# The opening stage of a two-layer decoder trunk: another order of its transfers, other sums of squares, and three products of zeros

## The chip, the cores and the metric

The kernel runs on one core of one Trainium2 chip. The metric is the device time of one execution in microseconds (us). Three runs of the kernel before took 1147.78, 1148.49 and 1148.76 us, so the median is 1148.49 us. The names of the engines are those of the profile: PE is TensorE (PEld its weight loads), DVE is VectorE, ACT is ScalarE, POOL is GpSimd, and SP is the engine whose queue issues the transfers here.

## What is computed

A sequence of 512 tokens of width 1024 goes through two layers. Both layers also attend to 256 fixed memory tokens, whose keys and values come from the normalised memory. Only the start of the computation is touched by the change:

```python
mem_n = rms_norm(mem, ln_mem)
for layer in range(DEPTH):
    h = rms_norm(x, ln_mix[layer])
    mkv = mem_n @ w_mem_kv[layer]
    mem_k = mkv[..., :MEM_W].reshape(b_sz, MEM_LEN, MEM_HEADS, MEM_DH)
    mem_v = mkv[..., MEM_W:].reshape(b_sz, MEM_LEN, MEM_HEADS, MEM_DH)
    if layer < N_A_LAYERS:
        mix_out, mem_q = gated_deltanet_mixer(h, gdn_w_in[a], gdn_conv[a], gdn_A_log[a], gdn_dt_bias[a], gdn_norm[a])
    else:
        ...
    x = x + jnp.concatenate([mix_out, mem_o], axis=-1) @ w_out[layer]
    x = x + swiglu(rms_norm(x, ln_ffn[layer]), w_gate_up[layer], w_down[layer])
```

Here `rms_norm(x, g)` is `x * rsqrt(mean(x * x) + eps) * g`. The gated-DeltaNet mixer needs, besides large projections of `h`, twelve narrow columns of `h` (the logits of its gates).

## The kernel before

Everything lies transposed: the width of 1024 is cut into eight blocks (k = 0 to 7) of 128 partitions, and tokens run along the free axis. `x` is 128x8x512 and `mem` 128x8x256. All large products work on pairs of fp32r tiles: a value is split into a rounded high part and the rest, and each product is done as three (high by high, low by high, high by low; `mm3`, line 206). Splitting a weight takes one ACT copy (`whi`) and one DVE subtraction (`wlo`, `split`, line 176). Splitting a block of memory takes an ACT copy with the gain as its scale (`mh`) and one DVE operation (`ml`, `split_gain`, line 180).

The opening stage is `mem_and_norm` (line 304), followed by `gates` (line 410). In it come, in this order of the program: the transfers, issued one after the other from SP's queue; the splits of the memory; `keys(0)` (48 products into the banks `pj`); the memory's root mean square; the same for `x`; `memory_columns`; `values(0)`; `keys(1)`; `values(1)` (48 products each); and `norm`, which scales `x` and splits it into `h` and `l`. The order within each engine is made by a scheduler from this order and the operations' needs, so an operation can be put ahead of others; once built, each engine takes its instructions strictly in that order.

The root mean squares are made by `rstd_of` (line 229): ACT squares each block into a tile `sq`, DVE adds the squares of two blocks, and PE multiplies each such sum by a tile of ones, accumulating four products in a bank `g`; ACT then takes a logarithm and an exponential of it (`rsqrt`, line 224) into `mr` (memory) or `xr` (x). These products are of plain fp32 tiles. The ones come with the constants, by a transfer that stands ahead of those of `x` (`fetch_constants`, line 297).

`norm` (line 372) does three operations for each k: DVE scales `x` in place by the gain and `xr`, ACT copies it into `h`, and DVE subtracts, which gives `l`. `gates` multiplies the scaled `x` by the narrow weights `wab`; ACT copies the result into `ab`, four small products of `ab` with a part of the constants turn it round into a bank `g`, and ACT and DVE make the gates from that (`z`, `l`, `gate`). After these come the projections of the mixer (`conv_tile`, line 464), which fill PE: 24 products 512 wide for each tile of weights.

Of the kernel before, what the change touches and what calls it, by code (L numbers as in the profile page):

```python
# [18 lines left out]
P = 128  # L19
# [26 lines left out]
C_ID, C_U, C_ONE, C_CAUS, C_BAND = 0, 128, 256, 384, 512  # L46
C_SEL, C_INV, C_SIGN = 768, 780, 781
C_N = 782
# [20 lines left out]
def constants():  # L69
# [4 lines left out]
    c[:, C_ONE:C_ONE + P] = 1.0  # L74
# [14 lines left out]
class Builder:  # L89
# [139 lines left out]
    def rstd_of(self, tiles, pool, out, after=None):  # L229

        ps = self.bank("g")[:, :tiles[0].shape[1]]
        for k in range(0, KD, 2):
            two = []
            for x in tiles[k:k + 2]:
                sq = self.t(pool, [P, x.shape[1]], F32, "sq", 6)
                two.append(sq)
                ins = self.square(sq, x)
                if after is not None:
                    self.nosync(ins, after)
            self.tt(self.nc.vector, two[0], two[0], two[1], ALU.add)  # L240
            self.mm(ps, self.ones, two[0], k == 0, k == KD - 2)
        self.rsqrt(out, ps, D)


# [33 lines left out]
    def load_constants(self, cp):  # L278
# [8 lines left out]
        self.ones = c[:, C_ONE:C_ONE + P]  # L287
        self.caus = c[:, C_CAUS:C_CAUS + P]
        self.band = c[:, C_BAND:C_BAND + 2 * P]
        self.one = c[:, C_ONE:C_ONE + 1]  # L290
# [13 lines left out]
    def mem_and_norm(self, ep):  # L304
# [5 lines left out]
        ml = self.t(ep, [P, KD, ML], F32R, "ml")  # L310
        self.use(LN_EXP)
        early = lambda src: self.load(src, ep, 6)
        raw = [self.t(ep, [P, D], F32, "wraw", 6)]
        for k in range(0, KD, 2):
            nc.sync.dma_start(mem[:, k:k + 2, :], a["memT"][:, k:k + 2, :])
            if k < 4:
                s = slice(k // 2 * T, (k // 2 + 1) * T)
                nc.sync.dma_start(raw[0][:, s], a["wmk"][0, 0][:, s])
        raw += [early(a["wmk"][0, 1])]
        self.fetch_constants()  # L320
# [4 lines left out]
        raw += [early(s) for s in (a["wmv"][0, 0], a["wmv"][0, 1])]  # L325
# [3 lines left out]
        raw += [early(s) for s in (a["wmk"][1, 0], a["wmk"][1, 1], a["wmv"][1, 0], a["wmv"][1, 1])]  # L329
        self.kept = {}  # L330
# [3 lines left out]
        mem_stats = lambda after: self.memory_stats(ep, mem, mr, after)  # L334

        def keys(layer):
            ps, ks = [], []
            for m in range(2):
                w = self.weight(None, nc.vector, raw[4 * layer + m], 1 if m + layer else 2)
                ps.append(self.bank("sc" if layer else "pj")[:, :ML])  # L340
                for k in range(KD):
                    self.mm3(ps[m], w, k, (mh[:, k, :], ml[:, k, :]), k == 0, k == KD - 1)
            if layer == 0:
# [947 lines left out]
```

## Time and profile before

| What | Value |
|---|---|
| Runs of the kernel before | 1147.78 to 1148.76 us, median 1148.49 us |
| Profiled execution: its own time | 1148.39 us |
| Profiled execution: span from first to last instruction | 1146.6 us |
| Instructions | 19668 |
| DVE, ACT, POOL busy over the span | 73%, 55%, 7% |
| Transfers | 152.83 MB, mean 133 GB/s |

The profiled execution is 0.10 us below the median, so sums made against its trace can be set against the median as they are. The span is 1.8 us shorter than the execution's own time; what lies around it is taken to stay. A row of the timeline gives the start in us, the time that the merged instructions took together, engine, line, operation, what is written and read, shapes, and how many instructions follow each other; a bracket tells how long the engine had been idle before and what ended that. A row of the busy times by stretch gives the stretch, its length, and for PE, PEld, DVE, ACT and POOL the busy time and the number of instructions, then the granted TensorE clock, the share of the DMA engines and their rate. Matmuls overlap, so what one product costs is the distance between two starts, not its own length.

In this profile the first transfer of the memory lands before 5.45 us, the first product starts at 6.92 us, and the products of the gates start at 40.53 us.

### The profile page before, as it was taken

Reading aid. Unit: us, or ns where it says so; the run is one execution under the profiler, and the core shown is the slowest. Engines: PE = TensorE matmul, PEld = TensorE weight load, DVE = VectorE, ACT = ScalarE, POOL = GpSimd, SP = SyncE. Lnnn points to the kernel's source line nnn. Section 1 sums busy time; section 2 is a strip of 40 time slices with the busy share of each in tenths; the row PEclk is TensorE's granted clock in tenths of the full one; section 3 lists DMA queues with packets and bytes.
Section 4 is the critical chain, followed back from the end, with each engine's and each line's share of the span. In section 5 each row is a group of like instructions: output and inputs, shape, how many; then the busy total and the mean of one; then the engine's idle time right before and its main releaser. Section 6 shows DMA issues by size and latency. Waiting matters only on the chain.

```text
span 1146.6 us, 19668 instructions
## 1 busy us (share of the span) xinstructions
PE 1127.0 (98%) x7476; PEld 990.7 (86%) x7476; DVE 841.2 (73%) x1587; ACT 631.5 (55%) x1271; POOL 86.0 (7%) x97
## 2 busy tenths in 40 slices
PE   7999999999999999999999999999999999999996
PEld 5888887887899998899998777778999988999986
DVE  5764887766789987489866777759699843898754
ACT  7579572366556652256654556765566522566533
POOL 0220000000101100011100000010011100111000
PEclk9999999999999999999999999999999999999999
DMA  8333342325657744567723411144477733577232
GB/s 312 124 116 108 123 107 97 99 86 166 175 142 190 189 125 125 151 151 182 184 74 101 138 56 56 56 111 129 105 191 188 187 108 106 141 191 185 70 96 93
DMA packets 73972, 152.83 MB, mean 133 GB/s; under 512 B 17757, under 2 KB 18421, under 8 KB 73877
## 3 DMA queue, kind: packets, MB, share of 16 engines
q1 hardware_dynamic: 62356, 130.59, 36.8%
q0 software_dynamic: 11520, 20.98, 11.6%
q8 instruction: 59, 0.97, 0.4%
q14 instruction: 37, 0.30, 0.1%
HBM read 144.58 MB, written 6.96 MB: 132 GB/s over the span
## 4 chain that ended last, share of the span: by engine, by line
PE 89%; DVE 5%; ACT 4%; DMA 1%; issue 1%; SPq 0%; DVEq 0%; ACTq 0%
PE pj L154 44%; PE g L154 38%; PE sc L154 6%; ACT sm L142 2%; DVE wlo L161 1%; PE g L158 1%; DMA wraw<-in_wmk 1%; DVE q L161 0%; DVE sm L784 0%; PE qk L154 0%; ACT sm L148 0%; DVE l L164 0%; ACT whi L148 0%; ACT pf L148 0%; DVE l L161 0%
## 5 line engine op out<-in xcount | busy, mean ns | idle before, releaser
L148 ACT ACTIVATE whi<-wraw 128x512 fp32r<-128x512 f32 (+2 forms) x331 | 243.9, 746 | 244.9 <-PE pj L154 151.8
L161 DVE TENSOR_TENSOR wlo<-wraw,whi 128x512 fp32r<-128x512 f32 (+2 forms) x331 | 274.8, 840 | 102.6 <-ACT whi L148 96.8
L154 PE MATMUL pj<-h,whi 128*128 128x512 f32 (+1 forms) x676 | 267.4, 397 | 0.2 <-ACT h L148 0.2
L154 PE MATMUL pj<-l,whi 128*128 128x512 f32 (+1 forms) x676 | 264.2, 391 | 0.6 <-DVE l L164 0.4
L154 PE MATMUL pj<-h,wlo 128*128 128x512 f32 (+1 forms) x676 | 264.0, 390 | 0.0
L154 PE MATMUL g<-T,whi 128*128 128x256 f32 x1280 | 228.1, 278 | 0.2
L154 PEld LDWEIGHTS g<-T,whi 128*128 128x128 f32 x1280 | 194.7, 188 | 1.8 <-DVE fu L164 1.8
L154 PE MATMUL g<-T,wlo 128*128 128x256 f32 x640 | 177.8, 278 | 0.0
L154 PEld LDWEIGHTS pj<-h,whi 128*128 128x128 f32 x676 | 126.8, 188 | 31.2 <-issue 5.8
L154 PEld LDWEIGHTS pj<-l,whi 128*128 128x128 f32 x676 | 127.1, 188 | 26.8 <-issue 1.1
L154 PEld LDWEIGHTS pj<-h,wlo 128*128 128x128 f32 x676 | 127.0, 188 | 25.7 <-issue 0.3
L154 PE MATMUL g<-h,whi 128*128 128x256 f32 (+1 forms) x508 | 144.5, 285 | 0.0
L154 PE MATMUL g<-h,wlo 128*128 128x256 f32 (+1 forms) x508 | 144.3, 284 | 0.0
L154 PE MATMUL g<-l,whi 128*128 128x256 f32 (+1 forms) x508 | 144.2, 284 | 0.0
L154 PEld LDWEIGHTS g<-T,wlo 128*128 128x128 f32 x640 | 120.1, 188 | 0.0
L154 PEld LDWEIGHTS g<-h,whi 128*128 128x128 f32 x508 | 95.3, 188 | 1.5 <-issue 0.3
L154 PEld LDWEIGHTS g<-l,whi 128*128 128x128 f32 x508 | 95.3, 188 | 1.2
L154 PEld LDWEIGHTS g<-h,wlo 128*128 128x128 f32 x508 | 95.3, 188 | 1.1
L1025 POOL DMA_DIRECT2D ws<-in_wgu x40 | 35.4, 885 | 693.6 <-DMA ws<-in_wgu 274.9
L148 ACT ACTIVATE whi<-ws 128x512 fp32r<-128x512 f32 x80 | 50.5, 631 | 49.0 <-PE g L154 40.2
L161 DVE TENSOR_TENSOR fu<-pj,rstd 128x512 f32<-128x512 f32 (+1 forms) x34 | 22.4, 660 | 54.5 <-PE pj L154 54.4
L161 DVE TENSOR_TENSOR wlo<-ws,whi 128x512 fp32r<-128x512 f32 x80 | 54.9, 686 | 6.4 <-ACT whi L148 6.3
(355 smaller groups left out, 1617.9 us busy)
## 6 DMA issues: line engine op xcount, KB each, us to landing
wraw<-in_wgu SPq DMA_DIRECT2D x48, 512.0 KB, 4.3
ws<-in_wgu SPq DMA_DIRECT2D x80, 256.0 KB, 3.5
ws<-in_wgu POOLq DMA_DIRECT2D x80, 256.0 KB, 4.8
wraw<-in_wdn SPq DMA_DIRECT2D x48, 384.0 KB, 3.1
wraw<-in_win SPq DMA_DIRECT2D x26, 512.0 KB, 3.6
wraw<-in_wgu SPq DMA_DIRECT2D x40, 256.0 KB, 4.2
wraw<-in_wout SPq DMA_DIRECT2D x16, 512.0 KB, 3.6
wraw<-in_wdn SPq DMA_DIRECT2D x16, 256.0 KB, 2.7
```

The costliest lines, as they stand in the source:

```text
L142: ins = self.nc.scalar.activation(out, in_, func, **kw).ins
L148: self.copied = self.nc.scalar.activation(out, in_, AF.Copy, **kw).ins
L154: return self.nc.tensor.matmul(out, lhsT, rhs, start=start, stop=stop, skip_group_check=more).ins
L158: return self.nc.tensor.transpose(out, in_, self.ident[:k, :k]).ins
L161: return eng.tensor_tensor(out=out, in0=a, in1=b, op=op).ins
L1025: nc.gpsimd.dma_start(s1, a22, accum_op=ALU.add)
```

## The change

The order of the transfers becomes: gains, memory and the two weights of `keys(0)` (the second now in two halves), the weights of `values(0)`, `x`, `wab`, the weights of the second layer, and then the constants. The tile of ones is written on the chip by DVE, and no longer lies in the constants.

The memory's squares are made by POOL, four products of a tile with itself, 128x512 each, into tiles `mq`; DVE adds them up with four additions, and one product by ones follows where four stood. The squares of `x` are made by ACT in four operations of 128x1024, DVE adds them with seven additions, and again one product by ones follows; this one is put into `keys(1)`, after its fourth block. `norm` multiplies `x` by `xr` on POOL for k = 0, 2, 4, 6, 7 and on DVE for k = 1, 3, 5; the gain moves into the split (an ACT copy with a scale, a DVE operation with `x`, gain and `h`) and, for the gates, into `wab`, by one POOL product. Three products of a zeroed tile, 512 wide and of plain fp32, are put on PE ahead of everything else; POOL writes the zeros.

```diff
-    def rstd_of(self, tiles, pool, out, after=None):
-
-        ps = self.bank("g")[:, :tiles[0].shape[1]]
-        for k in range(0, KD, 2):
-            two = []
-            for x in tiles[k:k + 2]:
-                sq = self.t(pool, [P, x.shape[1]], F32, "sq", 6)
-                two.append(sq)
-                ins = self.square(sq, x)
-                if after is not None:
-                    self.nosync(ins, after)
-            self.tt(self.nc.vector, two[0], two[0], two[1], ALU.add)
-            self.mm(ps, self.ones, two[0], k == 0, k == KD - 2)
-        self.rsqrt(out, ps, D)
...
-        self.ones = c[:, C_ONE:C_ONE + P]
+        self.ones = self.t(cp, [P, P], F32, "ones")
+        nc.vector.memset(self.ones, 1.0)
...
+        zero = self.t(ep, [P, 2, T], F32, "sq", 4)[:, 0, :]
+        nc.gpsimd.memset(zero, 0.0)
+        for _ in range(3):
+            self.mm(self.bank("g"), zero[:, :P], zero)
         self.use(LN_EXP)
         early = lambda src: self.load(src, ep, 6)
-        raw = [self.t(ep, [P, D], F32, "wraw", 6)]
+        raw = [self.t(ep, [P, D], F32, "wraw", 6) for _ in range(2)]
+        half = [slice(i * T, (i + 1) * T) for i in range(2)]
         for k in range(0, KD, 2):
             nc.sync.dma_start(mem[:, k:k + 2, :], a["memT"][:, k:k + 2, :])
             if k < 4:
-                s = slice(k // 2 * T, (k // 2 + 1) * T)
-                nc.sync.dma_start(raw[0][:, s], a["wmk"][0, 0][:, s])
-        raw += [early(a["wmk"][0, 1])]
-        self.fetch_constants()
+                nc.sync.dma_start(raw[0][:, half[k // 2]], a["wmk"][0, 0][:, half[k // 2]])
+        for s in half:
+            nc.sync.dma_start(raw[1][:, s], a["wmk"][0, 1][:, s])
+        raw += [early(s) for s in (a["wmv"][0, 0], a["wmv"][0, 1])]
         for k in range(KD):
             self.split_gain(mem[:, k, :], self.gain(G_MEM, k), mh[:, k, :], ml[:, k, :])
         for k in range(0, KD, 2):
             nc.sync.dma_start(x[:, k:k + 2, :], a["xT"][:, k:k + 2, :])
-        raw += [early(s) for s in (a["wmv"][0, 0], a["wmv"][0, 1])]
         wab = self.wab = self.t(ep, [P, KD, 32], F32, "wab")
         nc.gpsimd.memset(wab, 0.0)
         nc.sync.dma_start(wab[:, :, 0:12], a["wab"])
         raw += [early(s) for s in (a["wmk"][1, 0], a["wmk"][1, 1], a["wmv"][1, 0], a["wmv"][1, 1])]
+        self.fetch_constants()
...
-        mem_stats = lambda after: self.memory_stats(ep, mem, mr, after)
-
-        def keys(layer):
+
+        def summed(pairs):
+            for i, j in ((0, 1), (2, 3), (0, 2)):
+                self.tt(nc.vector, pairs[i], pairs[i], pairs[j], ALU.add)
+            return pairs[0]
+
+        def squares_of_memory():
+            pairs = []
+            for k in range(0, KD, 2):
+                sq = self.t(ep, [P, 2, ML], F32, "mq", 4)
+                self.tt(nc.gpsimd, sq, mem[:, k:k + 2, :], mem[:, k:k + 2, :], ALU.mult)
+                pairs.append(sq)
+            both = summed(pairs)
+            self.tt(nc.vector, both[:, 0, :], both[:, 0, :], both[:, 1, :], ALU.add)
+            return both[:, 0, :]
+
+        def squares_of_x():
+            pairs = []
+            for k in range(0, KD, 2):
+                sq = self.t(ep, [P, 2, T], F32, "sq", 4)
+                self.square(sq, x[:, k:k + 2, :])
+                self.tt(nc.vector, sq[:, 0, :], sq[:, 0, :], sq[:, 1, :], ALU.add)
+                pairs.append(sq[:, 0, :])
+            return summed(pairs)
+
+        def rstd_of(sq, out):
+            ps = self.bank("g")[:, :sq.shape[1]]
+            self.mm(ps, self.ones, sq)
+            self.rsqrt(out, ps, D)
+
+        def keys(layer, between=None):
             ps, ks = [], []
             for m in range(2):
-                w = self.weight(None, nc.vector, raw[4 * layer + m], 1 if m + layer else 2)
+                w = self.weight(None, nc.vector, raw[4 * layer + m], 1 if layer else 2)
                 ps.append(self.bank("sc" if layer else "pj")[:, :ML])
                 for k in range(KD):
                     self.mm3(ps[m], w, k, (mh[:, k, :], ml[:, k, :]), k == 0, k == KD - 1)
+                    if between is not None and m == 0 and k == 3:
+                        between()
             if layer == 0:
-                mem_stats(self.copied)
+                rstd_of(squares_of_memory(), mr)
...
         def norm():
             self.h, self.hx = [], [x[:, k, :] for k in range(KD)]
+            self.tt(nc.gpsimd, wab, wab, self.gains[:, G_MIX[0]:G_MIX[0] + KD].unsqueeze(2).to_broadcast([P, KD, 32]), ALU.mult)
             for k in range(KD):
                 self.h.append(self.pair(self.apool))
-                xk = x[:, k, :]
-                self.stt(xk, xk, self.gain(G_MIX[0], k), xr, ALU.mult, ALU.mult)
-                self.split(xk, *self.h[k])
+                self.tt(nc.vector if k in (1, 3, 5) else nc.gpsimd, x[:, k, :], x[:, k, :], xr, ALU.mult)
+                self.split_gain(x[:, k, :], self.gain(G_MIX[0], k), *self.h[k])
 
         self.memK = keys(0)
-        self.rstd_of([x[:, k, :] for k in range(KD)], ep, xr)
         self.memory_columns(mr, mc)
         self.memV = values(0)
-        keys(1)
+        keys(1, lambda: rstd_of(squares_of_x(), xr))
         values(1)
         norm()
-
-    def memory_stats(self, ep, mem, mr, after):
-        self.rstd_of([mem[:, k, :] for k in range(KD)], ep, mr, after=after)
```

The rest of the diff renumbers the columns of the constants and drops `memory_stats`. Behind the gates no row differs on any engine, but that one projection product stands behind the small products of the gates and not ahead of them, and that `ones` is read where `consts` was.

On DVE, ahead of the product that needs the first weights' low parts, the order was this (numbers behind a name are the program's; `raw[1]` of the first layer is split in one piece):

```order
L161 TENSOR_TENSOR wlo_141<-wraw_91,whi_140 128x512
L164 SCALAR_TENSOR_TENSOR ml_89<-mem_86,gains_67,mh_88 128x256 x4
L161 TENSOR_TENSOR wlo_172<-wraw_98,whi_171 128x1024
L161 TENSOR_TENSOR sq_201<-sq_201,sq_203 128x256
L161 TENSOR_TENSOR sq_207<-sq_207,sq_209 128x256
L161 TENSOR_TENSOR sq_213<-sq_213,sq_215 128x256
L161 TENSOR_TENSOR sq_219<-sq_219,sq_221 128x256
```

With the change the same place reads as follows; `wlo_183` belongs to the second weight of `keys(0)`, `wlo_238` and `wlo_242` to those of `values(0)`:

```order
L163 SCALAR_TENSOR_TENSOR ml_91<-mem_88,gains_67,mh_90 128x256 x4
L160 TENSOR_TENSOR wlo_183<-wraw_102,whi_182 128x512
L160 TENSOR_TENSOR mq_213<-mq_213,mq_215 128x512
L160 TENSOR_TENSOR wlo_183<-wraw_102,whi_182 128x512
L160 TENSOR_TENSOR mq_217<-mq_217,mq_219 128x512
L160 TENSOR_TENSOR mq_213<-mq_213,mq_217 128x512
L160 TENSOR_TENSOR wlo_238<-wraw_111,whi_237 128x1024
L160 TENSOR_TENSOR mq_213<-mq_213 128x256
L160 TENSOR_TENSOR wlo_242<-wraw_113,whi_241 128x1024
```

The additions of the memory's squares now stand between the halves of the second weight and ahead of the weights of `values(0)`. POOL, which had only memsets before the mixer's `DT`, now has these rows in the opening stage:

```order
L296 MEMSET sq_92 128x512
L315 MEMSET wab_135 128x256
L160 ISA
L160 TENSOR_TENSOR mq_213<-mem_88 128x512
L160 TENSOR_TENSOR mq_215<-mem_88 128x512
L160 TENSOR_TENSOR mq_217<-mem_88 128x512
L160 TENSOR_TENSOR mq_219<-mem_88 128x512
L160 TENSOR_TENSOR wab_135<-wab_135,gains_67 128x256
L160 TENSOR_TENSOR x_89<-x_89,xr_150 128x512 x5
```

So nine products of 128x512 and one of 128x256 are new on POOL, five of them in the stretch of `norm`. On DVE the rows of that stretch were these, where `x` is scaled on DVE alone and weights of the second layer (`wlo_354`, `wlo_390`, `wlo_394`) stand among them:

```order
L164 SCALAR_TENSOR_TENSOR x_87<-x_87,gains_67,xr_139 128x512
L161 TENSOR_TENSOR wlo_354<-wraw_131,whi_353 128x1024
L161 TENSOR_TENSOR l_460<-x_87,h_459 128x512
L164 SCALAR_TENSOR_TENSOR x_87<-x_87,gains_67,xr_139 128x512
L161 TENSOR_TENSOR wlo_390<-wraw_133,whi_389 128x1024
L161 TENSOR_TENSOR kt_382<-sc_328,mr_137 128x256
L161 TENSOR_TENSOR l_465<-x_87,h_464 128x512
L161 TENSOR_TENSOR wlo_394<-wraw_135,whi_393 128x1024
L164 SCALAR_TENSOR_TENSOR x_87<-x_87,gains_67,xr_139 128x512
```

With the change they are these; the first `x` is k = 1, the two together are k = 3 and 5, and `wlo_571` belongs to the first projection of the mixer:

```order
L160 TENSOR_TENSOR wlo_384<-wraw_142,whi_383 128x1024
L160 TENSOR_TENSOR kt_376<-sc_303,mr_148 128x256
L160 TENSOR_TENSOR x_89<-x_89,xr_150 128x512
L160 TENSOR_TENSOR wlo_388<-wraw_144,whi_387 128x1024
L163 SCALAR_TENSOR_TENSOR l_450<-x_89,gains_67,h_449 128x512
L160 TENSOR_TENSOR kt_380<-sc_351,mr_148 128x256
L163 SCALAR_TENSOR_TENSOR l_455<-x_89,gains_67,h_454 128x512
L163 SCALAR_TENSOR_TENSOR l_460<-x_89,gains_67,h_459 128x512
L160 TENSOR_TENSOR x_89<-x_89,xr_150 128x512 x2
L160 TENSOR_TENSOR wlo_571<-wraw_568,whi_570 128x1024
L163 SCALAR_TENSOR_TENSOR l_465<-x_89,gains_67,h_464 128x512
```

The three `l` of k = 0, 1, 2 stand ahead of `x` for k = 3 and 5. On ACT, ahead of the copy of the gates' product (`ab`), stood this:

```order
L148 ACTIVATE kt_422<-sc_397,mc_138 128x256
L148 ACTIVATE whi_612<-wraw_610 128x1024
L148 ACTIVATE h_484<-x_87 128x512
L148 ACTIVATE h_489<-x_87 128x512
L148 ACTIVATE kt_451<-pj_426,mc_138 128x256
L148 ACTIVATE ab_503<-pj_494 128x512
L148 ACTIVATE z_510<-g_505 128x24
```

And now this, where `h_464` is k = 3, `h_474` is k = 5 and `h_484` is k = 7:

```order
L147 ACTIVATE whi_570<-wraw_568 128x1024
L147 ACTIVATE h_464<-x_89,gains_67 128x512
L147 ACTIVATE kt_416<-sc_391,mc_149 128x256
L147 ACTIVATE h_469<-x_89,gains_67 128x512
L147 ACTIVATE h_474<-x_89,gains_67 128x512
L147 ACTIVATE h_479<-x_89,gains_67 128x512
L147 ACTIVATE h_484<-x_89,gains_67 128x512
L147 ACTIVATE kt_445<-pj_420,mc_149 128x256
L147 ACTIVATE whi_607<-wraw_605 128x1024
L147 ACTIVATE ab_498<-pj_489 128x512
L147 ACTIVATE whi_659<-wraw_657 128x1024
L147 ACTIVATE z_505<-g_500 128x24
```

Five `h`, from k = 3 on, and one more weight (`whi_607`) now stand ahead of `ab`, where two `h` stood.

More of the change, by code (lines that the diff above doesn't have):

```diff
@@ L43 @@
 G_N = G_GDN + 1
-C_ID, C_U, C_ONE, C_CAUS, C_BAND = 0, 128, 256, 384, 512
-C_SEL, C_INV, C_SIGN = 768, 780, 781
-C_N = 782
+C_ID, C_U, C_CAUS, C_BAND = 0, 128, 256, 384
+C_SEL, C_INV, C_SIGN = 640, 652, 653
+C_N = 654
 INV_FREQ = [float.fromhex(s) for s in (
@@ L286, in load_constants @@
         self.U = c[:, C_U:C_U + P]
-        self.ones = c[:, C_ONE:C_ONE + P]
+        self.ones = self.t(cp, [P, P], F32, "ones")
+        nc.vector.memset(self.ones, 1.0)
         self.caus = c[:, C_CAUS:C_CAUS + P]
         self.band = c[:, C_BAND:C_BAND + 2 * P]
-        self.one = c[:, C_ONE:C_ONE + 1]
+        self.one = self.ones[:, 0:1]
         v = self.t(cp, [P, 10], F32, "eps")
```

1 line of the change is left out of this document (removed).

## The prediction

> **What bounds the kernel now.** I read the page first, then the busy times by stretch over the first 60 us, then the timeline there, engine by engine.
>
> ```profile
> PE 1127.0 (98%) x7476; PEld 990.7 (86%) x7476; DVE 841.2 (73%) x1587; ACT 631.5 (55%) x1271; POOL 86.0 (7%) x97
> PE 89%; DVE 5%; ACT 4%; DMA 1%; issue 1%; SPq 0%; DVEq 0%; ACTq 0%
> ```
>
> PE is busy 98% of the span and makes 89% of the chain that ended last. The rest of the chain is in the start:
>
> ```profile
> 0.00:10.00 10.00, 3.08 (x13) 2.85 (x14) 4.19 (x12) 5.33 (x10) 0.52 (x5) 1.00 0.71 237
> 10.00:20.00 10.00, 9.24 (x51) 7.26 (x51) 5.59 (x11) 8.48 (x21) 0.00 (x0) 1.00 1.02 370
> 20.00:30.00 10.00, 9.80 (x65) 8.07 (x65) 8.28 (x12) 8.34 (x14) 0.00 (x0) 1.00 0.73 287
> 30.00:40.00 10.00, 10.00 (x86) 10.00 (x85) 10.00 (x16) 6.23 (x9) 2.37 (x3) 1.00 0.12 40
> 40.00:50.00 10.00, 10.00 (x61) 6.93 (x60) 5.64 (x13) 4.46 (x13) 2.66 (x1) 1.00 0.54 161
> 50.00:60.00 10.00, 10.00 (x48) 8.12 (x47) 7.01 (x9) 6.83 (x15) 5.20 (x4) 1.00 0.67 231
> ```
>
> From 30 us on PE is busy 10.00 of every 10.00 us, and behind the gates no row of any engine is moved. So I take the shift of PE at the gates as the shift of the end, one for one. Between 30 and 40 us DVE too is busy 10.00 of 10.00: whatever is added to DVE, or holds it up, reaches the gates soon.
>
> ```profile
> 6.92 0.58 PE L154 MATMUL pj<-mh,whi 128*128 128x256 f32 x1 [6.92 <-ACT whi L148]
> 10.81 0.41 PE L154 MATMUL pj<-ml,whi 128*128 128x256 f32 x1
> 11.02 0.41 PE L154 MATMUL pj<-mh,wlo 128*128 128x256 f32 x1
> 11.81 0.28 PE L154 MATMUL pj<-ml,whi 128*128 128x256 f32 x1
> 11.93 0.28 PE L154 MATMUL pj<-mh,wlo 128*128 128x256 f32 x1
> 16.03 3.83 PE L154 MATMUL g<-sq,consts 128*128 128x256 f32 x12
> 20.31 2.29 PE L154 MATMUL g<-sq,consts 128*128 128x512 f32 x4
> 22.03 0.68 PE L154 MATMUL pj<-whi,mh 128*128 128x256 f32 x1
> 28.92 0.28 PE L154 MATMUL sc<-mh,whi 128*128 128x256 f32 x1
> 40.53 1.92 PE L154 MATMUL pj<-x,wab 128*32 128x512 f32 x16
> 43.42 0.95 PE L154 MATMUL g<-consts,ab 128*128 128x12 f32 x8
> 42.60 0.60 ACT L148 ACTIVATE ab<-pj 128x512 f32<-128x512 f32 x1 [1.01 <-PE pj L154]
> ```
>
> These are my milestones: the first product at 6.92, `keys(0)` done at 16.03, `values(0)` from 22.03 to 28.92, the gates' products at 40.53, the turning of `ab` at 43.42. Starts lie 0.21 apart at 11 us and 0.12 at 12 us, though the granted clock reads 1.00: PE begins at about half pace.
>
> **What the change removes on PE.** Eight products by ones become two. The twelve rows at 16.03 are four products of 128x256 and two of 128x512 (two rows each), as much as eight of 128x256 in 3.83 us: 0.48 each at most, and 0.43 less the drain of the last and a short wait. I take 0.43, and 0.86 for 128x512 (the 2.29 for two, at 20.31, has a wait and the drain in it). Six fewer are 3 x 0.43 + 3 x 0.86 = 3.9 us. If the zeros bring PE to full pace before 6.92, the 21 products up to 11.45 save 0.09 each, 1.9 us. With the 0.8 us that PE waited for the second `wlo`, some 6 us could go at best. That holds only if nothing else is late.
>
> **What it adds: POOL.** POOL read no tensor in this stretch; now it multiplies nine times 128x512. The trace has such work only later, and there it disturbs DVE:
>
> ```profile
> 54.80 1.30 POOL L161 TENSOR_TENSOR DT<-gcr,consts 128x512 f32<-128x512 f32 x1 [9.46 <-DMA gcr<-dr]
> 56.05 1.30 POOL L161 TENSOR_TENSOR DT<-gcr,consts 128x512 f32<-128x512 f32 x1
> 57.29 2.30 POOL L161 TENSOR_TENSOR DT<-gcr,consts 128x512 f32<-128x512 f32 x1
> 52.26 1.23 DVE L161 TENSOR_TENSOR wlo<-wraw,whi 128x1024 fp32r<-128x1024 f32 x1 [2.19 <-ACT whi L148]
> 56.38 2.05 DVE L161 TENSOR_TENSOR wlo<-wraw,whi 128x1024 fp32r<-128x1024 f32 x1 [0.66 <-ACT whi L148]
> 58.35 2.30 DVE L164 SCALAR_TENSOR_TENSOR kn<-pj,gains,kn 128x511 f32<-128x511 f32 x3
> ```
>
> `wlo` takes 1.23 us alone and 2.05 beside POOL. It ended at 58.43; less 1.23 it began at 57.20, when POOL's second operation (56.05 to 57.35) was ending. POOL's third took 2.30 for 1.30: it ended at 59.59, so began at 58.29, when `wlo` was ending. So they did not run together: they took turns, each starting some 0.14 before the other's recorded end. I therefore charge each such operation its duration less 0.13 on one common path. The three `kn` behind it, each with one input in a PSUM bank (`pj`), took 0.75 as ever while POOL went on. So the second input in SBUF seems to be what matters. DVE's new operations (`ml`, `l`, the additions, `x` by `xr`) have both inputs in SBUF; for additions and `x` the nearest row is `wlo` itself, for the three-operand `ml` and `l` no row shows it.
>
> [...]
>
> The durations:
>
> ```profile
> L148 ACT ACTIVATE whi<-wraw x14: 612/1054/1063, 6.3 to 55.3; 128x1024 fp32r<-128x1024 f32 x12, 128x512 fp32r<-128x512 f32 x2
> L161 DVE TENSOR_TENSOR wlo<-wraw,whi x14: 692/1226/2052, 6.9 to 56.4; 128x1024 fp32r<-128x1024 f32 x12, 128x512 fp32r<-128x512 f32 x2
> L164 DVE SCALAR_TENSOR_TENSOR ml<-mem,gains,mh x8: 478/480/486, 6.0 to 10.5; 128x256 fp32r<-128x256 f32 x8
> L164 DVE SCALAR_TENSOR_TENSOR x<-x,gains,xr x8: 746/747/751, 25.4 to 39.1; 128x512 f32<-128x512 f32 x8
> L161 DVE TENSOR_TENSOR l<-x,h x8: 684/689/693, 27.2 to 41.5; 128x512 fp32r<-128x512 f32 x8
> L148 ACT ACTIVATE h<-x x8: 613/616/635, 26.2 to 40.6; 128x512 fp32r<-128x512 f32 x8
> 5.45 0.91 ACT L148 ACTIVATE mh<-mem,gains 128x256 fp32r<-128x256 f32 x2 [3.43 <-DMA mem<-in_memT]
> 27.09 0.47 ACT L148 ACTIVATE mv<-pj,mc 128x256 f32<-128x256 f32 x1 [0.22 <-PE pj L154]
> 22.64 0.69 ACT L142 ACTIVATE xr<-g,eps 128x512 f32<-128x512 f32 x1 [0.94 <-PE g L154]
> ```
>
> On the common path, in us: POOL 1.16; `wlo` 1.10, its half 0.56; `ml` 0.35; an addition or `x` by `xr` 0.56; the new `l`, a three-operand one like the old `x`, 0.62. Two operations in a row on ACT lie their length less 0.08 apart.
>
> **Step 1, keys(0).** From 5.4 (the memory's first transfer, not moved) to the last `ml` the path carries 4 x 1.16 (squares), 8 x 0.35 (`ml`) and 2 x 0.56 (`wlo` of the first weight) = 8.6, with the tail of the last and small gaps 14.3. PE finishes the first weight's products at 14.9 and needs 24 x 0.12 = 2.9 for the second: 17.9, not 16.03. The first step is 1.8 us late, and PE's pace does not matter in it, since PE waits for `ml` and `wlo`: the zeros gain nothing here.
>
> **Step 2, values(0).** DVE then has two halves, three additions of 0.6, and `wlo` of the values: 18.6; one short addition, 19.0. The product by ones lies at 19.0 to 19.45; behind it stand 43 products of 0.12 and 0.45 for the memory's columns: 25.1, where before it was 28.92. Now 3.9 us are gained.
>
> **Step 3, keys(1) and values(1).** In ACT's order the copy `mv` of the last values stands ahead of the next weight: 0.2 + 0.47 + 1.05 after 25.1 gives 26.7, two products, then `x`'s one product by ones to 27.85. The low part of the weight waits for DVE's additions of `x`'s squares (ACT, busy with `mr` and `mv`, ends the squares at 24.8, and DVE adds until 26.9), takes 1.2 and comes at 28.1; 94 products of 0.12 then run to 39.4; before, 40.53. Of the gain 1.1 is left, since PE stood still for 1.7.
>
> **Step 4, x by xr.** `xr` waits for that product: logarithm to 28.65, one `whi` in between (0.97), exponential 0.6: 30.15, the path free at 30.75. From there it carries five POOL products (5.8), `x` for k = 1, 3, 5 (1.7), one `wlo` (1.1) and three `l` (1.85): 10.4, to 41.2. `x` of k = 3 comes at 40.8, of k = 5 at 41.4.
>
> **Step 5, ab.** ACT waits for k = 3. Then stand there five `h` (5 x 0.53), two `kt` (2 x 0.39), one `whi` (0.97), `ab` (0.62): 5.0, to 45.85. PE turns `ab` at 45.9, where before it was 43.42: **2.4 us later**. The 15 projections behind it (3.4) cover the gates' small chain (some 3.2 with `whi`, `wlo`, `z`). No more is lost, nothing regained.
>
> The transfers are not on this path: the memory and first weight keep their places, and constants, now last, are first read at the turning of `ab`; `x` can come 1.5 us later than before (18.5 for the last) without a change, as ACT squares it after 20. POOL's product on `wab`, half as large as the others, falls at about 20 us and costs DVE one short turn, if any. The memset of ones and the three products of zeros lie before 6.92, where PE and DVE waited. Sum: 1148.39 + 2.4 = **1150.8 us**. If the overlap of turns is 0.2 and not 0.13, steps 1 and 4 gain 1.2; if it is only 0.08, they lose 1.1. So the forecast's own range is 1149.5 to 1152.0.
>
> **Rivals.**
>
> *`ml` and `l` do not block* (only two-input operations without a scalar do). For it: no row shows them blocked. Against: they read two SBUF inputs at the same pace as `wlo`. Step 1 then ends at 15.1, `xr` comes at 27.4; the path carries 5.8 + 1.7 + 1.1 = 8.6 from 28.0, so `x` of k = 5 comes at 36.8; three `h`, `kt`, `whi` and `ab` give 40.4, and 0.6 goes at the gates, where `wlo` stands ahead of `z`. Result 2.4 faster, 1146.0 (1145.1 to 1147.9).
>
> *Nothing blocks*, POOL runs free, and the change does all that its words say: gates at 36.2, turning at 38.9; 4.6 faster, 1143.8. The 2.05 speaks against it.
>
> *DVE goes first* whenever it has an operation ready, so POOL waits. No row shows DVE with two such operations in a row beside POOL. Then `x` of k = 6 and 7 comes last, behind DVE's six `l` and `wlo` (13.4 on the path from 31.1: 45.0), with `h`, `kt`, `whi` and `ab` behind: 47.6, 4.0 later, 1152.4. It decides as soon as POOL's last `x` falls behind k = 5.
>
> *PE stays at or falls back to half pace* up to 18 us, because between 7 and 12 us it now waits more than it works: the second weight's products then take 5 and not 2.9; some of that falls into waits, and 1.1 is added: 1151.9.
>
> [...]
>
> **Numbers.** Chances: forecast 0.40, DVE first 0.16, half pace 0.10, `ml` and `l` free 0.27, nothing blocks 0.07. A measurement of this kernel can tell some 0.2%, 2.3 us, from no change: the bounds are 1146.1 and 1150.7. Half of the forecast lies above (0.20), with DVE first (0.16) and most of half pace (0.08): slower 0.44. Half of the forecast, the slower part of the first rival (0.11) and 0.02: same 0.33. The rest, 0.16 + 0.07, faster 0.23. The range takes in the forecast, both slower rivals and the first rival: 1145.2 to 1152.7; it leaves out mainly that nothing blocks.
>
> **What would show it.** In the changed profile `ml` and `l` with a mean well above 0.48 and 0.75 where POOL works, `wlo` up to 2.3: the common path. `keys(0)` done at about 18 tells step 1; `values(0)` done at 25 step 2; PE idle some 1.7 behind it step 3; POOL's five `x` stretched over about 9 us instead of 6.3, step 4; `ab` at 45 and idle PE ahead of the turning, step 5. I am wrong if `l` beside POOL takes 0.75, or if the gates come before 38; and I am wrong in the carrying over if PE idles somewhere behind 60 us.

## The result, and the profile after

| | before | changed |
|---|---|---|
| Median of four runs each | 1148.13 us | 1155.03 us |
| Lowest to highest | 1147.38 to 1148.76 | 1153.37 to 1156.12 |
| Ratio to before, 95% interval | | 1.0059 [1.0042, 1.0077] |
| Profiled execution: own time, span | 1148.39, 1146.6 us | 1153.37, 1151.5 us |

The change makes the kernel 6.9 us slower. The direction was forecast, the size was not: 1150.8 was given, with 1145.2 to 1152.7 as the range. The profiled execution is the fastest of the changed kernel's four, so its trace shows 5.0 of the 6.9 us.

The page first: busy times and the chain that ended last.

```profile
PE 1131.3 (98%) x7470; PEld 992.5 (86%) x7470; DVE 846.1 (73%) x1587; ACT 629.7 (55%) x1260; POOL 101.7 (9%) x108
PE 84%; DVE 8%; ACT 5%; issue 2%; DMA 1%; SPq 0%; DVEq 0%; ACTq 0%
```

PE's busy time grew by 4.3 us (1127.0 before), but the three products of zeros alone are 5.0 of that (first row of PE's timeline below), so the totals don't tell the cause. In the chain PE's share fell from 89% to 84% and DVE's rose from 5% to 8%: the end waits more for DVE. The stretches (busy time of PE, PEld, DVE, ACT and POOL, then the granted clock) say where:

```profile
10.00:20.00 10.00, 9.05 (x53) 8.70 (x54) 9.40 (x15) 4.89 (x8) 1.98 (x2) 0.70 1.05 395
40.00:50.00 10.00, 7.54 (x35) 4.58 (x30) 7.44 (x11) 6.46 (x11) 4.47 (x4) 0.83 0.43 133
```

The column of the granted clock, 1.00 in all six stretches before, falls to 0.70 between 10 and 20 us and to 0.83 between 40 and 50. PE is busy only 7.54 us of the latter, where it was 10.00 before. The timeline of PE shows both places:

```profile
1.32 5.01 PE L153 MATMUL g<-sq 128*128 128x512 f32 x6 [1.32 <-POOL sq L296]
...
11.96 0.58 PE L153 MATMUL pj<-ml,whi 128*128 128x256 f32 x1 [0.84 <-DVE ml L163]
...
18.62 0.59 PE L153 MATMUL g<-mq,ones 128*128 128x256 f32 x2
...
26.59 0.39 PE L153 MATMUL sc<-mh,whi 128*128 128x256 f32 x1 [1.51 <-ACT whi L147]
...
39.51 3.10 PE L153 MATMUL pj<-x,wab 128*32 128x512 f32 x16
...
46.06 1.34 PE L153 MATMUL g<-consts,ab 128*128 128x12 f32 x8 [2.32 <-ACT ab L147]
47.25 0.77 PE L153 MATMUL pj<-l,whi 128*128 128x512 f32 x1
47.82 0.63 PE L153 MATMUL pj<-h,wlo 128*128 128x512 f32 x1
...
49.95 0.46 PE L153 MATMUL pj<-l,whi 128*128 128x512 f32 x1
...
52.20 0.40 PE L153 MATMUL g<-consts,gate 128*24 128x128 f32 x2
...
61.31 0.66 PE L157 MATMUL g<-consts,kn 128*128 128x128 f32 x4
...
169.26 1.14 PE L153 MATMUL sc<-pf,mv 128*64 128x128 f32 x16 [0.56 <-ACT pf L147]
```

The milestones stand close to the forecast up to the turning of `ab`: product by ones 18.62 (forecast 19.0), first product of the next weight 26.59 (26.7), gates 39.51 (39.4), turning 46.06 (45.9). Then they part. Behind the turning the starts lie 0.43 apart (five products in the 2.13 from 47.82 to 49.95), where they lay 0.23 apart before (14 steps from 44.55 to 47.76). The products of `gate` stand at 52.20, before at 48.08: 2.64 late had become 4.12. (One projection product fewer stands ahead of them than before and follows behind them, so `kn`, at 61.31 for 56.92, is 4.39 late.) PE's rows of the kernel before at this place:

```profile
44.55 0.40 PE L154 MATMUL pj<-h,wlo 128*128 128x512 f32 x1
...
47.76 0.39 PE L154 MATMUL pj<-l,whi 128*128 128x512 f32 x1
48.08 0.40 PE L154 MATMUL g<-consts,gate 128*24 128x128 f32 x2
...
56.92 0.66 PE L158 MATMUL g<-consts,kn 128*128 128x128 f32 x4
```

DVE and POOL show what the prediction called the common path:

```profile
7.62 2.44 DVE L163 SCALAR_TENSOR_TENSOR ml<-mem,gains,mh 128x256 fp32r<-128x256 f32 x2
...
11.43 1.66 DVE L163 SCALAR_TENSOR_TENSOR ml<-mem,gains,mh 128x256 fp32r<-128x256 f32 x4
...
34.85 1.79 DVE L163 SCALAR_TENSOR_TENSOR l<-x,gains,h 128x512 fp32r<-128x512 f32 x1
...
39.97 1.28 DVE L160 TENSOR_TENSOR x<-x,xr 128x512 f32<-128x512 f32 x2
...
42.31 3.39 DVE L163 SCALAR_TENSOR_TENSOR l<-x,gains,h 128x512 fp32r<-128x512 f32 x5
...
51.95 0.18 DVE L163 SCALAR_TENSOR_TENSOR gate<-gate,ea 128x24 f32<-128x24 f32 x1
```

```profile
5.38 1.04 POOL L160 TENSOR_TENSOR mq<-mem 128x512 f32<-128x512 f32 x1 [3.87 <-DMA mem<-in_memT]
...
30.30 9.20 POOL L160 TENSOR_TENSOR x<-x,xr 128x512 f32<-128x512 f32 x5 [10.39 <-ACT xr L141]
```

`ml` took 1.22 each beside POOL's squares (two in 2.44) and 0.42 to 0.48 without them (four in 1.66); `l` took 1.79 beside POOL's `x`, and 0.68 each later. POOL's five products took 9.20 together, 1.84 each, where the first square took 1.04. So both sides wait. ACT, in turn, stood 5.04 us for `x` of k = 3, and later 2.30 for a transfer, with `z` behind it, so that `gate` was done only at 52.13 (51.95 and 0.18, last row of DVE above):

```profile
40.69 0.72 ACT L147 ACTIVATE h<-x,gains 128x512 fp32r<-128x512 f32 x1 [5.04 <-DVE x L160]
...
48.31 1.06 ACT L147 ACTIVATE whi<-wraw 128x1024 fp32r<-128x1024 f32 x1 [2.30 <-DMA wraw<-in_win]
49.27 0.17 ACT L147 ACTIVATE z<-g 128x24 f32<-128x24 f32 x1
```

### The profile page after: what moved, and what is told of

It reads as the page before. It is cut to its first block, busy times and chain, and to the rows that moved or that the text cites. A ratio compares the mean times of both kernels' runs of the same rounds, so it can differ in the third digit from the quotient of the medians.

```text
span 1151.5 us, 19664 instructions
## 1 busy us (share of the span) xinstructions
PE 1131.3 (98%) x7470; PEld 992.5 (86%) x7470; DVE 846.1 (73%) x1587; ACT 629.7 (55%) x1260; POOL 101.7 (9%) x108
## 4 chain that ended last, share of the span: by engine, by line
PE 84%; DVE 8%; ACT 5%; issue 2%; DMA 1%; SPq 0%; DVEq 0%; ACTq 0%
PE pj L153 40%; PE g L153 37%; PE sc L153 5%; ACT sm L141 2%; DVE wlo L160 2%; DVE l L163 1%; DVE btmp L160 1%; ACT whi L147 1%; DVE big L160 1%; ACT sm L147 1%; PE g L157 1%; DVE q L160 0%; DVE sm L799 0%; PE qk L153 0%; DMA big<-basein 0%
```

## The experiments

Each compares with runs of the kernel before on the same chip; "now" and "the changed kernel" in the expectations mean the changed kernel.

**POOL's reads, one by one and together.** Three kernels take POOL's products away, in `norm`, in the squares of the memory, and in both.

```diff
-                self.tt(nc.vector if k in (1, 3, 5) else nc.gpsimd, x[:, k, :], x[:, k, :], xr, ALU.mult)
+                self.tt(nc.vector, x[:, k, :], x[:, k, :], xr, ALU.mult)
```

> All eight products of x by xr go on DVE, POOL keeps the memory's squares. Theory (DVE and POOL take turns on operands in SBUF, and ACT, the gates and the chain behind ab are late because x of k = 3 and 5 is): from 31 us on l takes 0.75 each and wlo 1.2, the last x comes at about 42.3 (eight x of 0.6, six l of 0.66, one wlo and one kt from 31.3), ab is turned at about 43.7 and not at 46.06, ACT no longer stands idle for 5 us before h of k = 3, and the time falls by some 4 us against the changed kernel, to about 1151. Rival (DVE has simply too much to do there, the turns with POOL are not the cause): DVE has three more us of work, ab is turned after 47 and the time rises to 1157 or more.

Measured 1150.46 us, 1.0018 [1.0009, 1.0027]. DVE (first fence) and PE of this kernel:

```profile
39.72 0.75 DVE L163 SCALAR_TENSOR_TENSOR l<-x,gains,h 128x512 fp32r<-128x512 f32 x1
...
42.02 0.68 DVE L160 TENSOR_TENSOR x<-x,xr 128x512 f32<-128x512 f32 x1
```

```profile
44.50 1.06 PE L153 MATMUL g<-consts,ab 128*128 128x12 f32 x8
...
57.84 0.66 PE L157 MATMUL g<-consts,kn 128*128 128x128 f32 x4
...
166.08 1.14 PE L153 MATMUL sc<-pf,mv 128*64 128x128 f32 x16 [0.82 <-ACT pf L147]
```

With eight products on DVE in place of three, `l` takes 0.75, and the last `x` comes at 42.70 (42.02 and 0.68): 0.4 later than expected, and 1.45 later than DVE's last in the changed kernel (39.97 and 1.28). Yet `ab` is turned 1.56 earlier, at 44.50, since ACT is not held up by k = 3 with all its other work behind it: only one `h` and `ab` are left to it behind the last `x`. That order is new too. The scheduler, given this edit, also put projection products between those of the gates on PE, so what is gained belongs to the five products and the new order together. The rival, a turning after 47, is out. Turning and the transpositions of `kn` are late by 1.08 and 0.92 against before (43.42, 56.92): carried one to one, with no wait of 2.3 us in front. Another 1.16 went in two waits further on (0.82 here, 0.34 at 214.54), of which more below.

```diff
-                self.tt(nc.gpsimd, sq, mem[:, k:k + 2, :], mem[:, k:k + 2, :], ALU.mult)
+                self.square(sq, mem[:, k:k + 2, :])
```

> The memory's squares go on ACT, POOL keeps five products of x by xr. Theory (turns with POOL made keys(0) late): ml takes 0.48 each, the product by ones comes before 17 (now 18.8), values(0) ends near 23 (now 25.1), xr comes 2 us earlier, ab is turned near 44, and the time falls by 2 to 3 us against the changed kernel, to 1152 to 1153. Rival (the half pace of PE until 15.75 us, not POOL, made keys(0) late): ml is short, but products still lie 0.21 apart until 15 or so, and less than 1 us is gained. Second rival: what is gained at values(0) is lost again, since x by xr decides: ab turned at 46 as now, 1155.

Measured 1151.65 us, 1.0034 [1.0022, 1.0045], a little below the 1152 to 1153 expected. PE, and the stretch from 10 to 20 us:

```profile
15.95 0.64 PE L153 MATMUL g<-mq,ones 128*128 128x256 f32 x2
...
43.46 1.06 PE L153 MATMUL g<-consts,ab 128*128 128x12 f32 x8 [2.32 <-ACT ab L147]
...
45.20 0.63 PE L153 MATMUL pj<-h,whi 128*128 128x512 f32 x1
45.62 0.63 PE L153 MATMUL pj<-l,whi 128*128 128x512 f32 x1
...
58.66 0.66 PE L157 MATMUL g<-consts,kn 128*128 128x128 f32 x4
```

```profile
10.00:20.00 10.00, 9.43 (x71) 8.93 (x71) 9.55 (x16) 7.99 (x14) 0.62 (x1) 1.00 1.05 394
```

The product by ones comes at 15.95, the granted clock stays at 1.00, and `ab` is turned at 43.46: within 0.04 of the kernel before. Yet the kernel is 3.5 us slower than before. This row is the one that convicts the prediction's last step: the same 2.32 us of waiting ahead of the turning, products 0.43 apart behind it, and `kn` at 58.66 instead of 56.92 (1.3 of the span's growth to 1149.7 lies further on). A kernel that turns `ab` on time still loses what lies behind.

Both edits together:

> Both edits: no square of the memory and no x by xr on POOL. Theory: the two gains add, ab is turned near 41.5, the time is 1148 to 1149, at or a little above the kernel before; the rest of the new head is then worth nothing or 1 us. Rival (turns are not the cause): 1155 or more, as DVE and ACT have more work.

Measured 1147.54 us, 0.9996 [0.9987, 1.0005], a little below the expectation. The turning is 1.36 earlier than before:

```profile
42.06 1.06 PE L153 MATMUL g<-consts,ab 128*128 128x12 f32 x8
```

All that the changed kernel loses hangs on POOL's nine products of 128x512. Without them the new head is as fast as the old one, within what can be measured. That they do their harm by taking turns with DVE is what the rows of `ml`, `l` and POOL show; no kernel here has the products without the turns.

**The zeros.** Taken out of the changed kernel, and put alone into the kernel before.

```diff
-        zero = self.t(ep, [P, 2, T], F32, "sq", 4)[:, 0, :]
-        nc.gpsimd.memset(zero, 0.0)
-        for _ in range(3):
-            self.mm(self.bank("g"), zero[:, :P], zero)
```

> The changed kernel without the three products of zeros (and without the memset of their tile). Theory (PE waits for ml and wlo up to 14 us, so its pace does not matter there): first products 0.21 apart, all else where it was, keys(0) at 18, the time within 0.6 us of the changed kernel. Rival (the zeros warm PE to good purpose): keys(0) is 1 us later or more, the time 1 to 2 us longer. Second rival (the zeros bring the fall back of the clock forward, without them full pace starts earlier than 15.75): keys(0) before 17.5, the time 0.5 to 1 shorter.

Measured 1153.92 us, 1.0051 [1.0039, 1.0064]: its interval overlaps that of the changed kernel, with the middle 1 us below. The theory is not contradicted, a small cost of the zeros is not excluded.

```profile
18.41 0.59 PE L153 MATMUL g<-mq,ones 128*128 128x256 f32 x2
...
47.86 0.63 PE L153 MATMUL pj<-h,wlo 128*128 128x512 f32 x1
...
52.12 0.63 PE L153 MATMUL pj<-h,whi 128*128 128x512 f32 x1
```

The product by ones at 18.41 (18.62 with zeros): nothing is lost in the start without them. The same kernel shows a longer second stretch at half pace: products 0.43 apart from 47.86 to 52.12 at least, 4.3 us, where the profiled run of the changed kernel had 2.1.

> The kernel before with only the three products of a zeroed tile (and POOL's memset) put ahead. Theory (products lie 0.12 apart from 6.9 on, but the first weight's products end with the last ml at 11 and the second's wait for wlo until 13.3, so pace is worth little): 0.1 to 0.6 us faster than before, within 0.1%. Rival (pace matters): 1.5 to 2 us faster, about 1146.3. Rival (as in the changed kernel, PE falls back to half pace by 10 us because it waits too much): no gain at all or up to 1 us slower.

Measured 1148.11 us against 1148.45 on the same chip, 0.9997 [0.9988, 1.0006].

```profile
39.94 1.92 PE L154 MATMUL pj<-x,wab 128*32 128x512 f32 x16
```

The gates come at 39.94 for 40.53, 0.6 earlier, and that is all the zeros can do there.

**What lies behind the turning.** Two things end there at nearly the same time: 15 projections at half pace, and the gates' chain behind ACT's wait. Three kernels separate them. `fill` puts eight products into PE's wait (the other products are held at their places); `z_first` only changes the order of two operations; `fill_z` does both.

```diff
+        own = [self.mm(pt, self.h[0][0][:, :P], self.h[0][0]) for _ in range(8)]
         for c in range(NC):
-            self.mm(pt[:, c * 12:(c + 1) * 12], ab[:, c * P:(c + 1) * P], sel)
+            own.append(self.mm(pt[:, c * 12:(c + 1) * 12], ab[:, c * P:(c + 1) * P], sel))
+        self.pin[4] = own
```

> The changed kernel with eight more products of h by itself (128x512) on PE, into the bank that the turning of ab overwrites, between the fourth projection and the turning: 1.8 us of work in the 2.3 us in which PE waited. The order of every engine is otherwise the changed kernel's. In the changed kernel two things end together behind the turning: 15 projections at half pace (until 52.2) and the gates' chain (gate at 52.1, as ACT's z stands behind whi, which waits for a transfer until 48.3). Theory (both bind, each hides the other): projections 0.23 apart at once, but PE then waits over 1 us for the gate, whose products stay at 52.2; the profiled time is that of the changed kernel, 1153 to 1154, and only its slower runs go, so the median falls from 1155 by 1 to 1.5. Rival (the clock alone): the gate's products come at 50.7, median 1152 to 1152.5. Rival (the clock is not behind it): projections still 0.43 apart, no change.

Measured 1151.54 us, 1.0025 [1.0014, 1.0036], 3.5 below the changed kernel.

```profile
46.90 1.06 PE L154 MATMUL g<-consts,ab 128*128 128x12 f32 x8 [0.51 <-ACT ab L148]
47.82 0.48 PE L154 MATMUL pj<-l,whi 128*128 128x512 f32 x1
...
51.44 0.40 PE L154 MATMUL g<-consts,gate 128*24 128x128 f32 x2
```

The 15 projections take 3.62 (47.82 to 51.44) and not 4.95, and PE does not wait at the gate, which DVE had done just before, at 51.18:

```profile
51.00 0.18 DVE L164 SCALAR_TENSOR_TENSOR gate<-gate,ea 128x24 f32<-128x24 f32 x1
```

In this run the head up to the turning was 0.84 later than in the changed kernel's profiled run (46.90 for 46.06), and it is still 1.8 us shorter.

For `z_first`, `hold` is the copy into `z`, and `ins` the copy of the third weight:

```diff
-        self.copy(hi, src)
+        ins = self.copy(hi, src)
+        if self.hold is not None:
+            self.weights += 1
+            if self.weights == 3:
+                self.nosync(ins, self.hold)
```

> The changed kernel with ACT's z ahead of the third projection's whi (which waits for its transfer), and with the DVE operation that belongs to it moved likewise; PE, POOL and the transfers in the same order. Theory (both bind): z at 47.5, the gate ready by 49.7, but PE comes to the gate's products at 52.2 as before, as its 15 projections run at half pace; time within 0.5 us of 1155. Rival (the chain alone, the clock's pace being a result and not a cause): the gate's products at 50.7 or earlier, 1.5 us or more gained.

Measured 1154.94 us, 1.0054 [1.0041, 1.0067]: nothing. ACT's `z`, and PE:

```profile
47.52 0.19 ACT L149 ACTIVATE z<-g 128x24 f32<-128x24 f32 x1 [1.62 <-PE g L156]
```

```profile
47.33 0.78 PE L156 MATMUL pj<-l,whi 128*128 128x512 f32 x1
...
53.67 0.40 PE L156 MATMUL g<-consts,gate 128*24 128x128 f32 x2
```

`z` is 1.75 earlier (47.52 for 49.27), but the products of `gate` stand at 53.67: the 15 projections took 6.34.

> Both edits of fill and z_first. Theory (both bind): only now do the gate's products come early, at 50.7 or so, and the time falls to 1152 (3 below the changed kernel, of which 1.5 is the gate's and 1.5 the slower runs'). Rivals: the clock alone, the same as fill; the chain alone, the same as z_first.

Measured 1151.39 us, 1.0024 [1.0015, 1.0033]: the same as `fill`. My theory, that both bind and each hides the other, fell; the rival "the clock alone" holds. In `fill` the chain through `z` was done 0.26 before PE came. This depends on when ACT's transfer lands: in the changed kernel's profiled run it landed late and `gate` was done at 52.13, so PE at full pace, there by 50.87 (47.25 and 3.62), would have had to wait. In the four other traces with half pace behind the turning the chain was ready 0.9 to 3.4 us before PE came (`squares_act`, `warm_keys`, `no_zeros`, `z_first`), and there the pace alone binds.

**The first fall of the clock.** Eighteen small products between the first weight's, in the waits for `ml`.

```diff
                     self.mm3(ps[m], w, k, (mh[:, k, :], ml[:, k, :]), k == 0, k == KD - 1)
+                    if layer == 0 and m == 0 and k < 6:
+                        for _ in range(3):
+                            self.mm(spare, mh[:, k, 0:P], mh[:, k, :])
```

> The changed kernel with eighteen more products on PE (three of 128x256, of mh by itself into a bank that is free, behind each of the first six blocks of the first weight): 0.12 each, 2.2 us of work in the waits for ml between 7 and 12 us. All other orders are the changed kernel's. Theory (PE does not wait from 12 us on, so that the half pace until 15.75 does cost: 16 products by 0.09 are 1.5 us, of which DVE's last sum, ready at 17.7, lets 0.9 through): products 0.12 apart throughout, the product by ones at 17.7 or 17.8 and not 18.6, ab turned 0.9 earlier, time 0.5 to 1.2 below 1155. Rival (the prediction's step: PE waits, its pace is worth nothing): the product by ones at 18.6, no change.

Measured 1152.25 us (1150.25 to 1154.27), 1.0033 [1.0021, 1.0045].

```profile
17.96 0.67 PE L153 MATMUL g<-mq,ones 128*128 128x256 f32 x2
...
45.71 1.06 PE L153 MATMUL g<-consts,ab 128*128 128x12 f32 x8 [2.33 <-ACT ab L147]
46.62 0.48 PE L153 MATMUL pj<-l,whi 128*128 128x512 f32 x1
...
47.94 0.63 PE L153 MATMUL pj<-h,whi 128*128 128x512 f32 x1
```

The pace stays full (1.00 granted from 10 to 20 us), the product by ones comes at 17.96 (0.66 earlier), but the turning only 0.35 earlier, at 45.71. By this pair of runs the prediction's step was nearer to the truth than my 0.9; by another pair, `fill` and the next kernel, which adds these products to `fill`, the turning comes 0.89 earlier (46.90 and 46.01). The median fell by 2.8, more than either; what the profiled run shows beside the 0.35 is a second stretch at half pace that begins late: the five products from 46.62 to 47.94 take 1.32, full pace with a slow start, and only from 47.94 on they lie 0.43 apart. Runs of this kernel differ by 4 us, and the clock goes with them: the mean granted clock over a whole run was 0.997 and 0.998 in the two fastest (1150.25 and 1150.46), as in the kernel before, 0.995 in the profiled one and 0.992 in the slowest (1154.27). How much of the 2.8 belongs to the edit stays open.

> warm_keys and fill together: PE kept busy in both stretches in which it waited. Theory (the two losses add): about 0.9 below fill's 1151.5, 1150.6, which is then what POOL's turns alone cost. Rival: 1151.5 as fill.

Measured 1150.58 us, 1.0021 [1.0012, 1.0030].

```profile
46.01 1.06 PE L154 MATMUL g<-consts,ab 128*128 128x12 f32 x8 [0.50 <-ACT ab L148]
...
50.51 0.40 PE L154 MATMUL g<-consts,gate 128*24 128x128 f32 x2
...
59.58 0.66 PE L158 MATMUL g<-consts,kn 128*128 128x128 f32 x4
```

In the start this run still fell to 0.90 between 10 and 20 us; behind the turning it did not fall (1.00 from 40 to 60). The turning at 46.01 is 2.59 late against before, the gate 2.43, `kn` 2.66: nothing is added behind it. The time is 2.4 above the 1148.19 measured beside it.

**A version that beats both.** From `no_pool_reads`, with the gates taken off the path: `xr` is one factor for each token, so it can be applied to the result for the gates instead of to `x`.

```diff
+            self.gps = self.bank("pj")
+            for k in range(KD):
+                s = slice(32 * (k % 4), 32 * (k % 4 + 1))
+                self.mm(self.gps[s, :], wab[:, k, :], x[:, k, :], k < 4, k >= 4)
...
-        self.copy(ab, ps)
+        self.tt(nc.vector, ab, self.gps, self.xr, ALU.mult)
```

> No POOL product on memory or x (as in no_pool_reads), and the gates taken off the path through x by xr: their products read the raw x while PE waits ahead of keys(1), and DVE multiplies the 128x512 result by xr in place of ACT's copy into ab (xr is one factor for each token, so it may be applied behind the product). ab is turned right behind the values, the low part of the first projection's weight stands ahead of x of k = 3 or later on DVE, and the gate's products stand behind the 16th projection or later. Theory (what was left late in no_pool_reads is DVE's chain x, l, wlo ahead of the gates: ab turned at 42.1, first wlo product at 41.5): ab turned before 39, the 28th projection 3 us earlier than there, time 1144 to 1145.5. Rival (DVE's l bind, whatever the order): 1147 as before. Rival (PE waits thinly between 37 and 44, the clock falls back again): 1148 or more, with a wider spread.

Measured 1144.54 us, 0.9969 [0.9956, 0.9981]: as expected.

```profile
37.17 0.95 PE L156 MATMUL g<-consts,ab 128*128 128x12 f32 x8
```

The turning is at 37.17. PE waits twice further on, 1.58 us at 161.01 and 1.35 at 210.51, in this profiled run, which took 1146.03; the other four took 1143.96 to 1144.61 and have no trace.

> early_gates without the three products of zeros. Theory (zeros move the gates by at most 0.6 us, as in the kernel before): within 0.7 us of early_gates. Rival (with no waits for POOL the zeros pay): 1.5 to 2 us longer.

Measured 1143.07 us, 0.9958 [0.9944, 0.9971], the fastest of all: 5.4 below before. The rival, that the zeros pay here, is out. The theory missed too: 1.47 below `early_gates` is more than its 0.7, so the zeros seem to cost something here, of which the traces place 0.5.

```profile
36.63 0.95 PE L156 MATMUL g<-consts,ab 128*128 128x12 f32 x8
```

The first product starts at 6.75, not at 7.24 as with zeros, and the turning is 0.54 earlier.

## Why the prediction was wrong

**Step 1, keys(0): the number held, half of its working did not.** The product by ones came at 18.62 (19.0 given for it in step 2). The last product of the second weight started at 17.89, and 17.9 was forecast; but two errors cancelled there, which is luck. The last `ml` ended at 13.09, not 14.3: the first square took POOL 1.04 (first row of POOL above), and the sum had charged it like `DT`, with its 1.30; four times 0.26 are most of the 1.2. And PE, after its last wait (up to 11.96), worked at half pace up to 15.75, 0.21 for each product and not 0.12. "PE's pace does not matter in it" was therefore wrong as a mechanism; it cost 0.66 at the product by ones and 0.35 at the turning (`warm_keys`). That the zeros gain nothing was right (`no_zeros`, `before_zeros`).

**Steps 2 to 4 held.** Turns between POOL and DVE for `ml` and `l` are the point on which forecast and first rival differed. No row of the kernel before shows them; charging them was my estimate. Measured: 1.22 for 0.48, 1.79 for 0.75. `x` of k = 3 released ACT at 40.69 (40.8). DVE did not go first: POOL's last `x` ended at 39.50, ahead of DVE's for k = 3 at 39.97.

**Step 5 failed in its last sentence.** The turning came at 46.06, for 45.9. "The 15 projections behind it (3.4) cover the gates' small chain. No more is lost": the 15 took 4.95 (47.25 to 52.20) in the fastest run, and some 6.3 in another (47.33 to 53.67, `z_first`, whose PE order is the same). The chain was mis-sized as well: 3.2 was given for it, and it took 6.07 (46.06 to 52.13) in the changed kernel's profiled run and 3.80 to 5.20 in `warm_fill`, `warm_keys`, `fill`, `no_zeros` and `squares_act`, where `z` stands at the same place. The cause of the lost pace is the 2.32 us in which PE stood still ahead of the turning: with eight products in it (`fill`) the granted clock reads 1.00 from 40 to 60 us, and 0.83 from 40 to 50 without them. I had forecast that wait, named it as a sign, and carried its length one to one, without asking what it does to PE's clock. `fill` gives it a price of 3.5 us in the median; `squares_act` shows it with a turning that is on time. The traces place 3.2 of it where the half pace was long (`z_first`: turning and 15 projections 7.71 from 45.96 to 53.67, where `fill` has 4.54), and 1.6 in the changed kernel's fastest run (6.14), where the late `gate` would have taken most of that as well. The rival "half pace" was priced for the first stretch alone.

**The sum, term by term.** Turns and the late chain: 2.4 forecast, 2.4 measured with both waits filled (`warm_fill`). That these agree so well is in part luck, as `warm_fill` still fell to 0.90 in its start and carries 26 products more. The clock: 0 forecast; filling both waits gave 4.4 back (1155.03 less 1150.58), 3.5 of it by the wait ahead of the turning. The missing term is larger than the whole forecast. One addition among the rivals is off: in *DVE goes first*, 31.1 and 13.4 make 44.5, not 45.0; the forecast doesn't hang on it.

**"I am wrong in the carrying over if PE idles somewhere behind 60 us"**: it did, by 0.56 at 169.26. With 4.39 at `kn` (61.31 for 56.92) that makes up the 4.9 by which the span grew.

A wait of 2.32 or 2.33 us was enough for half pace behind it in four of four profiled runs that had it with nothing put in (0.83 granted between 40 and 50 us in `after` and `squares_act`, 0.82 in `no_zeros` and `z_first`), and in `warm_keys` with a delay (0.89, then 0.94 between 50 and 60). In the first 60 us the granted clock reads 0.50 in eleven stretches of nine traces, and each lasts 3.4 or 6.8 us. What sets these lengths is not shown.

## What to carry to other kernels

When an estimate makes PE wait for as long as it did here, allow for a slower pace behind the wait besides its length: filling this wait of 2.32 us gave 3.5 back. Look for small products that can stand in the wait; `z_first`, which only shortened the chain behind it, gave nothing. And moving five products of 128x512 to POOL relieved DVE of little: its last `x` ended at 41.25, and at 42.70 where DVE does all eight (`x_all_dve`). Beside each other DVE's `l`, which reads two SBUF tiles, took 1.79 and not 0.75, POOL's product 1.84 where the first square took 1.04, and whoever waited for either got both delays.

## What the hardware showed beyond expectation

- The clock fell behind waits that are not long: behind 2.3 us in all five traces that had them, and behind the 1.51 ahead of the product at 26.59 in none of the ten that have this wait (1.00 granted from 20 to 40 us). In the changed kernel's start it fell where waits of 0.3 to 0.8 lie between short groups of products (0.70 granted between 10 and 20 us); with 18 more products in these waits it stayed at 1.00 in the run of `warm_keys`, and fell to 0.90 in that of `warm_fill`.
- When the fall began varied, and how long it lasted came in two sizes. The granted clock reads 0.50 for 3.4 us (46.7 to 50.1 in the changed kernel, 44.6 to 48.0 in `squares_act`, 47.7 to 51.1 in `warm_keys`) or for 6.8 (46.4 to 53.2 in `z_first` and in `no_zeros`, 9.2 to 16.0 in the changed kernel's start). In `squares_act` it fell 1.1 us behind the end of the wait, in `warm_keys` 2.0, after five projections at full pace; what sets the delay is not shown, and no kernel here moved the wait on purpose. Idle time alone is not the measure: in the changed kernel PE stood still for 2.3 of the 3.4 us before the fall at 46.7, and for 1.2 of the 3.4 before the one at 9.1. The six runs of `warm_keys` lie 4.0 us apart, the eleven of `warm_fill`, which has no wait of 2.3 us there, 1.1.
- The granted clock did not show every slow stretch of PE: in `no_zeros` it reads 1.00 from 10 to 20 us, while products start 0.21 apart up to 15.50 and 0.12 apart behind it. The distance between starts showed it.
- POOL and DVE delayed each other in both directions, and for operations with a scalar and two SBUF tiles as for plain ones: `wlo` (in the kernel before) went from 1.23 to 2.05, `l` went from 0.75 to 1.79, and POOL's 1.04 and 1.30 (square, `DT`) to 1.84.
- Waits of PE for ACT near 165 and 212 us, 0.2 to 1.6 us each, come and go between kernels whose order there is the same. They explain 0.6 of the changed kernel's loss and 1.2 of `x_all_dve`'s; what sets them off was not tried.
